# Hybrid decoder layer on one core: prompt attention issued in a fixed order on TensorE, with four smaller edits in the MLP

## The chip, the core and the metric

The kernel runs on one core of a Trainium2 chip. The metric is device time in microseconds, from the first to the last instruction and what lies around them; lower is better. The engines are TensorE (PE in the profile; its weight loads are PEld), VectorE (DVE), ScalarE (ACT), GpSimd (POOL) and SyncE (SP), whose queue issues the DMAs here.

## The reference, cut to what matters

One decoder layer is computed for a prompt of 2048 tokens and for a sample group of 8 x 8 tokens with a cache, width 1024, all in fp32. Half of the mixing is dilated attention of 8 heads of 64, in three branches (window 128 with stride 1, 512 with 4, 2048 with 16), which are merged by their softmax denominators; the other half is an RWKV-7 recurrence. Then come an output projection and an MLP.

```
n = rms_norm(x);  proj = n @ w_in
for w, d in ((128, 1), (512, 4), (2048, 16)):       # in dilated_attention
    s = q . k * scale + bias                        # keys at stride d
    mx = max(s);  e = exp(s - mx);  dn = sum(e);  o = e @ v
mall = max over branches of mx
num = sum(exp(mx - mall) * o);  den = sum(exp(mx - mall) * dn)
att = num / den
h = x + [att | rwkv] @ w_out
y = h + relu(rms_norm(h) @ w_mlp1)^2 @ w_mlp2
```

## The kernel before

The program has four stages: projections and RWKV (to some 1207 us), prompt attention (to some 1600), output projection beside the sample group's attention (to 1898), and the MLP. Apart from queues and dependencies, a list scheduler that simulates a timeline sets the order of each engine's instructions at build time: the program's order is its input, and it may put a ready instruction ahead of one that waits.

**Attention.** `attention(p, pump, ahead)` takes a pair of heads at a time, p = 0 to 3, and in it branches b = 0 to 2 and blocks of 128 queries, two at a time in branches 0 and 1 and four at a time in branch 2: 8 + 8 + 4 steps a pair. In a step, for each of the two heads `ty`: score products in two parts (`kst` and `klo`, lines 1084 and 1085, into `sc`), on VectorE a reduction that adds the bias and finds the maximum (line 1087, into `e` and `st`), the exponential on ScalarE (helper line 185), four transposes on TensorE (`pt`, line 1102), their evacuation to `pts` by `evac` (lines 1000 to 1005, in turn ScalarE and VectorE), and products with V into `o` (line 1109), which two steps (one in branch 2) share and ScalarE evacuates into `ob`.

**Merge.** `merge(p, ob, st)` is a generator. `pump()` drives it, which attention calls after each step of the next pair. It makes masked copies of the statistics on GpSimd (`zst`, `mv`, lines 1132 and 1133), brings them into rows by TensorE products (lines 1141, 1146, 1152) and ScalarE copies (`sw`), computes the branch weights on VectorE (`nall`, `scw`, `dn`, a reciprocal in line 1179), splits them into `wh` high and low, writes them to DRAM (`wD`, line 1187) and reads them back as `wrow` (line 1190). Twelve products (line 1197) spread the weights, VectorE multiplies `ob` by them, and GpSimd adds (line 1200; VectorE for the last pair). In the last pair's merge `sc` takes the place of `ax` in the names.

```
        def pump():
            for _ in range(2):
                next(before, None)
```

**MLP.** Three groups g of tokens, eight rounds r each. A round is `first` (line 1557) and `second` (line 1603), with products of high and low parts of both operands. `parts` (line 1477) splits a weight panel: `wh` on ScalarE, `wl` on VectorE, or on GpSimd where it is told so (`pooled`). `square_sums` (line 1410) squares the residual, adds on VectorE and sums by a TensorE product (line 1419) for the norm; four of its 24 calls stand at the end of group 0's round 0. `reload` fetches the next group's residual, and `normed(g + 1)` makes its scaled activations (`rl`, `mh`, `ml`) beside `second` of round 7.

Of the kernel before, what the change touches and what calls it, by code (L numbers as in the profile page):

```python
# [17 lines left out]
P = 128  # L18
# [153 lines left out]
def _build(ctx, tc, nc, I, O, dbg, upto):  # L172
# [879 lines left out]

    def attention(p, pump, ahead):
# [5 lines left out]
        for b in range(3):  # L1059
            bts = ahead.pop(("bias", p, b))  # L1060
            if p < 3:
                if b == 1:
                    ahead["kq", p + 1] = kq_load(p + 1)
                    coming = ahead["kq", p + 1][1]
                if b:
                    ahead["bias", p + 1, b - 1] = bias_load(p + 1, b - 1)
            vt = None
            for grp in range(4):
                vp, vt = vt, next_v()
                o = ppo.tile([P, 512], F32, name="o")  # L1070
                for t2 in range(0, 4, 2 if b < 2 else 4):
                    tl = [grp * 4 + t2 + i for i in range(2 if b < 2 else 4)]
                    w = 512 // len(tl)
                    work = []
                    for ty in range(2):
                        kst, klo, qst = K[ty]
                        ps = psc.tile([P, 512], F32, name="sc")
                        e = ae.tile([P, 512], F32, name="e", bufs=4)
                        blocks = []
                        for x, i in enumerate(tl):  # L1080
                            both = b < 2 and not (i == 0 if b == 0 else i < 4)
                            n = 256 if both else 128
                            c0 = x * w + w - n
                            PE.matmul(ps[:, c0:c0 + n], cols(qst, b, i, False), cols(kst, b, i, both), start=True, stop=False)  # L1084
                            PE.matmul(ps[:, c0:c0 + n], cols(qst, b, i, False), cols(klo, b, i, both), start=False, stop=True)  # L1085
                            nm, dn = st[:, 0, b, i // 4, ty, i % 4:i % 4 + 1], st[:, 1, b, i // 4, ty, i % 4:i % 4 + 1]
                            V.tensor_tensor_reduce(out=e[:, c0:c0 + n], in0=ps[:, c0:c0 + n], in1=bts[ty][:, 256 - n:256], scale=-1.0, scalar=3e38, op0=ALU.add, op1=ALU.min, accum_out=nm)
                            act(e[:, c0:c0 + n], e[:, c0:c0 + n], AF.Exp, bias=nm, scale=-1.0, accum_out=dn)
                            for hb in range(n // P):
                                old = n // P - 1 - hb  # L1090
                                if b == 0:
                                    kv = vt[:, i % 4 - old] if i % 4 >= old else vp[:, 3]
                                else:
                                    kv = (vp if old else vt)[:, i % 4]
                                blocks.append((i, kv, c0 + hb * P, hb == 0, hb == n // P - 1))
                        work.append((e, blocks))
                    ptss = []
                    for e, blocks in work:
                        pt = ppt.tile([P, 512], F32, name="pt")
                        pts = at.tile([P, 512], F32, name="pts", bufs=4)  # L1100
                        for y, (i, kv, c0, fst, lst) in enumerate(blocks):
                            PE.transpose(pt[:, y * P:(y + 1) * P], e[:, c0:c0 + P], ident)  # L1102
                        nb = len(blocks)
                        evac(pts[:, :nb * P], pt[:, :nb * P])
                        ptss.append(pts)
                    for y in range(nb):
                        for ty in range(2):
                            i, kv, c0, fst, lst = work[ty][1][y]
                            PE.matmul(o[ty * 64:ty * 64 + 64, (i % 4) * P:(i % 4 + 1) * P], kv[:, ty * 64:ty * 64 + 64], ptss[ty][:, y * P:(y + 1) * P], start=fst, stop=lst, tile_position=(0, ty * 64))  # L1109
                    pump()  # L1110
                    next(coming, None)
                if b == 0:
                    act(ob[b][:, grp * 512:(grp + 1) * 512], o, AF.Copy)
                elif b == 1:
                    act(ob[b][:, grp * 512:(grp + 1) * 512].rearrange("p (n q) -> p n q", q=4), o.rearrange("p (q n) -> p n q", q=4), AF.Copy)
                else:
                    act(ob[b].rearrange("p (m r) -> p m r", r=16)[:, :, grp * 4:(grp + 1) * 4], o.rearrange("p (r m) -> p m r", r=4), AF.Copy)
        for _ in coming:
            pass
        if p < 3:  # L1120
            ahead["bias", p + 1, 2] = bias_load(p + 1, 2)
        return merge(p, ob, st)

    def merge(p, ob, st):
# [13 lines left out]
        for x in range(2):  # L1138
            for g in range(4):
                c0 = x * 96 + g * 8  # L1140
                PE.matmul(ps[32 * g:32 * g + 32, x * P:x * P + P], flat[:, c0:c0 + 32], ident, start=True, stop=True, tile_position=(0, 32 * g))
        for x in range(2):
            for q in range(4):
                for g in range(4):
                    c0 = 256 + x * P + q * 32
                    PE.matmul(ps[32 * g:32 * g + 32, c0:c0 + 32], zst[:, x, q, g], rr1, start=True, stop=True, tile_position=(0, 32 * g))
# [3 lines left out]
        for g in range(4):  # L1150
            for ty in range(2):
                PE.matmul(ps[32 * g:32 * g + 32, 0:256], d2[:, g, ty], mv2[:, ty].rearrange("p x g c m -> p (x g c m)"), start=(ty == 0), stop=(ty == 1), tile_position=(0, 32 * g))
# [38 lines left out]
        yield  # L1191
        yield
        for g in range(4):
            cs = slice(g * 512, (g + 1) * 512)
            for b in range(3):
                ps = mp()
                PE.matmul(ps, wsel[:, g], wr[:, b], start=True, stop=True)
# [212 lines left out]
    def square_sums(h, i, c, ps, pl):  # L1410
# [7 lines left out]
        tt(sa[:, 0], sa[:, 0], sa[:, 1], ALU.add)  # L1418
        PE.matmul(ps[:SQ, 0:1], sa[:, 0], ones[:, 0:1], start=True, stop=True)
# [6 lines left out]
    with pool(name="wo2", bufs=1) as wo2, pool(name="pwo", bufs=4, space=PSUM, side="right") as pwo, pool(name="psa", bufs=1, space=PSUM) as psa, pool(name="pst", bufs=1, space=PSUM) as pst:  # L1426
# [5 lines left out]
        for c0 in range(0, NT, NC_):  # L1432
# [25 lines left out]
            if c0 + NC_ < NT:  # L1458
                for i in range(NC_ // SQ):
                    square_sums(h, c0 // SQ + i, i * SQ, pst.tile([P, 512], F32, name="pst"), wo2)  # L1460
    ph3.close()
    mw = ph4.enter_context(pool(name="mw", bufs=2))
# [5 lines left out]
    with pool(name="mm", bufs=1, side="right") as mm, pool(name="pm", bufs=8, space=PSUM) as pm:  # L1468
# [23 lines left out]
        def tmp():  # L1492
            return mw.tile([P, HT], F32, name="rl", bufs=12)
# [6 lines left out]
        def normed(g, h, mb):  # L1500
# [3 lines left out]
            dg = mw.tile([P, 8, SQ], F32, name="dg2", bufs=1)  # L1504
# [108 lines left out]
        for g in range(3):  # L1613
            late = []
            nh = None
            for r in range(8):
# [57 lines left out]
```

## Time and profile before

| | us |
|---|---|
| median of 3 runs | 3356.25 |
| lowest, highest | 3349.73, 3358.73 |
| the profiled execution | 3357.47 |
| its span | 3355.7 |
| TensorE busy in the span | 3135.5 (93%) |
| VectorE, ScalarE, GpSimd busy | 2157.2, 1469.2, 976.1 |
| mean granted TensorE clock | 0.965 |

Times in views count from the span's start. A busy total joins overlapping instructions of one engine; TensorE's products are pipelined, so the step from one start to the next is what one costs, not its duration. "idle before" names what released an engine after it had stood still.

### The profile page before, as it was taken

To read this page: it belongs to the slowest core of one execution; us is meant where nothing else is said; L and a number is where in the kernel's file an instruction comes from. 1 tells how busy PE (TensorE), PEld (TensorE's weight loads), DVE (VectorE), ACT (ScalarE), POOL (GpSimd) and SP (SyncE) were. 2 spreads that over 40 slices of the span, in tenths; PEclk is the share of its full clock that TensorE was granted. 3 is DMA by queue.
4 is the path that set the end of the run, shared out by engine and by line. 5 is a ranking of instruction groups with operands and counts; after the bars stand their busy time and mean duration, and the time that the engine had idled before them with its cause. 6 is when DMAs were issued, how large, how long until landed. Compare 5 with 4: busy or idle time off the path is not lost.

```text
span 3355.7 us, 63761 instructions
## 1 busy us (share of the span) xinstructions
PE 3135.5 (93%) x24214; PEld 2865.0 (85%) x24214; DVE 2157.2 (64%) x4547; ACT 1469.2 (44%) x3497; POOL 976.1 (29%) x1141
## 2 busy tenths in 40 slices
PE   5999899989988979999799689999999999999999
PEld 5876877877787868888688579999899999899999
DVE  4656677677566435656554577676976767967675
ACT  4545566555555446677222233232433323433332
POOL 1003422453044100111000233343533334533332
PEclk9999999999998989999899789999999999999999
DMA  5465575466456383323766322222232222222222
GB/s 169 137 185 149 131 204 158 109 157 178 124 131 178 106 279 117 126 74 90 243 221 235 123 85 89 64 85 64 98 113 64 88 63 86 88 68 84 64 89 73
DMA packets 349144, 418.55 MB, mean 125 GB/s; under 512 B 117252, under 2 KB 210367, under 8 KB 348837
## 3 DMA queue, kind: packets, MB, share of 16 engines
q1 hardware_dynamic: 348836, 414.48, 41.6%
q8 instruction: 190, 3.11, 0.4%
q14 instruction: 118, 0.96, 0.1%
HBM read 325.62 MB, written 93.46 MB: 125 GB/s over the span
## 4 chain that ended last, share of the span: by engine, by line
PE 72%; DMA 9%; DVE 9%; SPq 3%; issue 2%; POOL 2%; ACT 2%; DVEq 0%; POOLq 0%; ACTq 0%
PE pm L1603 20%; PE pm L1557 17%; PE pj L334 7%; PE pwo L1451 5%; PE pj L802 4%; PE o L1109 3%; PE pt L1102 2%; PE sc L1084 2%; PE sc L1085 2%; DVE ml L182 2%; DMA wr<-in_wq 1%; DMA wr<-in_wr 1%; DVE rl L1517 1%; DVE wl L1477 1%; DMA xg<-in_xg 1%
## 5 line engine op out<-in xcount | busy, mean ns | idle before, releaser
L185 ACT ACTIVATE wh<-wr 128x512 fp32r<-128x512 f32 x744 | 463.4, 625 | 818.5 <-PE pm L1603 473.4
L1603 PE MATMUL pm<-fh,wl 128*128 128x352 f32 x1536 | 495.9, 323 | 8.8 <-DVE wl L1477 8.8
L1603 PE MATMUL pm<-fh,wh 128*128 128x352 f32 x1536 | 493.4, 324 | 0.0
L1603 PE MATMUL pm<-fl,wh 128*128 128x352 f32 x1536 | 492.6, 323 | 0.5 <-DVE fl L182 0.5
L1557 PE MATMUL pm<-ml,wh 128*128 128x352 f32 x1344 | 437.0, 325 | 15.1 <-DVE ml L182 15.1
L1557 PE MATMUL pm<-mh,wh 128*128 128x352 f32 x1344 | 438.6, 327 | 9.4 <-ACT mh L185 9.2
L1557 PE MATMUL pm<-mh,wl 128*128 128x352 f32 x1344 | 436.0, 325 | 5.7 <-DVE wl L1477 4.6
L182 DVE TENSOR_TENSOR res<-pm,res 128x352 f32<-128x352 f32 x384 | 198.6, 522 | 287.5 <-PE pm L1603 284.7
L1477 DVE TENSOR_TENSOR wl<-wr,wh 128x512 fp32r<-128x512 f32 x432 | 361.1, 836 | 6.1 <-ACT wh L185 3.5
L1603 PEld LDWEIGHTS pm<-fh,wl 128*128 128x128 f32 x1536 | 290.2, 189 | 9.8 <-DVE wl L1477 9.8
L1603 PEld LDWEIGHTS pm<-fl,wh 128*128 128x128 f32 x1536 | 289.4, 189 | 1.3 <-DVE fl L182 1.1
L1603 PEld LDWEIGHTS pm<-fh,wh 128*128 128x128 f32 x1536 | 289.2, 189 | 0.8 <-ACT fh L185 0.2
L1557 PEld LDWEIGHTS pm<-ml,wh 128*128 128x128 f32 x1344 | 256.5, 191 | 19.1 <-DVE ml L182 19.0
L1557 PEld LDWEIGHTS pm<-mh,wh 128*128 128x128 f32 x1344 | 256.2, 191 | 11.5 <-ACT mh L185 11.5
L1557 PEld LDWEIGHTS pm<-mh,wl 128*128 128x128 f32 x1344 | 255.8, 190 | 8.9 <-DVE wl L1477 7.3
L802 PE MATMUL pj<-wh,nh 128*128 128x256 f32 (+1 forms) x816 | 242.4, 298 | 13.5 <-ACT qn L185 6.7
L802 PE MATMUL pj<-wh,nl 128*128 128x256 f32 (+1 forms) x816 | 241.1, 296 | 2.2 <-DVE nl L182 2.2
L334 PE MATMUL pj<-nh,wh 128*128 128x512 f32 (+3 forms) x600 | 222.8, 374 | 20.4 <-ACT nh L185 10.4
L1481 POOL TENSOR_TENSOR wr<-wr 128x512 f32<-128x512 f32 x48 | 68.9, 1435 | 591.0 <-DVE wl L1477 502.6
L802 PE MATMUL pj<-wl,nh 128*128 128x256 f32 (+1 forms) x816 | 240.7, 296 | 0.0
L182 DVE TENSOR_TENSOR wl<-wr,wh 128x512 fp32r<-128x512 f32 (+1 forms) x216 | 150.2, 698 | 135.2 <-ACT wh L185 130.0
L334 PE MATMUL pj<-nl,wh 128*128 128x512 f32 (+3 forms) x600 | 222.0, 371 | 5.9 <-DVE nl L182 5.9
(312 smaller groups left out, 7262.2 us busy)
## 6 DMA issues: line engine op xcount, KB each, us to landing
wr<-in_w SPq DMA_DIRECT2D x384, 256.0 KB
wr<-in_wr SPq DMA_DIRECT2D x120, 256.0 KB
wr<-in_wq SPq DMA_DIRECT2D x96, 256.0 KB
kv<-in_kc SPq DMA_DIRECT2D x40, 512.0 KB
kv<-in_vc SPq DMA_DIRECT2D x40, 512.0 KB
xsD<-xst SPq DMA_DIRECT2D x56, 256.0 KB
xrkv<-xsD SPq DMA_DIRECT2D x32, 384.0 KB
vt<-vD SPq DMA_DIRECT2D x48, 256.0 KB
```

The costliest lines, as they stand in the source:

```text
L182: V.tensor_tensor(out, a, b, op)
L185: S.activation(out, in_, func, bias=bias, scale=scale, **kw)
L334: PE.matmul(ps[:m, :n], a[:, k, :m], b[h * 4 + k][:, c0:c0 + n], start=(h == 0 and i == 0), stop=(h == 1 and i == 11))
L802: PE.matmul(out, a[h * 2 + k][:, i * P:i * P + m], b[:, k, :], start=(h == 0 and q == 0 and i % 2 == 0), stop=(h == 3 and q == 5 and (i % ...
L1084: PE.matmul(ps[:, c0:c0 + n], cols(qst, b, i, False), cols(kst, b, i, both), start=True, stop=False)
L1085: PE.matmul(ps[:, c0:c0 + n], cols(qst, b, i, False), cols(klo, b, i, both), start=False, stop=True)
L1109: PE.matmul(o[ty * 64:ty * 64 + 64, (i % 4) * P:(i % 4 + 1) * P], kv[:, ty * 64:ty * 64 + 64], ptss[ty][:, y * P:(y + 1) * P], start=fst, ...
L1451: PE.matmul(ps[:, :NC_], a[k][:, o * P:(o + 1) * P], b, start=(i == 0), stop=(i == 3 * KT - 1))
L1477: (G if pooled else V).tensor_tensor(wl, w, wh.bitcast(F32), ALU.subtract)
L1481: G.tensor_tensor(S[0], A21, A22, ALU.add)
L1557: PE.matmul(ps, a[:, k], b[:, k], start=(n == 0), stop=(n == 11))
L1603: PE.matmul(ps, a[:, f], b[:, cs], start=(i == 0), stop=(i == 11))
```

## The change

1. TensorE's instructions of the attention and the merge are issued in the program's order (`mul` and `turned`). The program now keeps a line of steps: a step's scores are issued three steps (LAG) ahead of its transposes and products with V. A step is: transposes of the step three back, `pump()`, scores of this step, `o` of the step three back, `pump()`. `e` has 6 buffers for 4. `pump()` takes one step of the merge, not two, and is called twice as often. For pairs 0 to 2 the merge yields four times, not twice, between issuing `wrow` and its first product, once for the last pair; there the line is emptied ahead of the merge.
2. ScalarE evacuates one `pt` in four, not one in two; VectorE the others.
3. The four late calls of `square_sums` are cut in two: squares and additions in round 0, TensorE's product and what follows in round 1. The `sq`, `rl` and `dg2` tiles move to a pool of their own, `mt`. `reload` comes at round 2, not 1.
4. In round 7 of groups 0 and 1, `second` makes its eight `wl` on GpSimd.

```
-        if evac.n % 2 in (0,):
+        if evac.n % 4 == 0:
...
+    def mul(*a, **k):
+        tc.keep_in_program_order(PE.matmul(*a, **k))
+    def turned(*a, **k):
+        tc.keep_in_program_order(PE.transpose(*a, **k))
+    line = []
+    def finish(step):
+        b, grp, ob, first, last, work, ptss = step
...
+        for y in range(len(work[0][1])):
+            for ty in range(2):
...
+                mul(o[ty * 64:ty * 64 + 64, ...], kv[:, ty * 64:ty * 64 + 64], ptss[ty][:, y * P:(y + 1) * P], ...)
...
+    def turn(step):
+        for e, blocks in step[5]:
+            pt = ppt.tile([P, 512], F32, name="pt")
+            pts = at.tile([P, 512], F32, name="pts", bufs=4)
+            for y, (i, old, c0, fst, lst) in enumerate(blocks):
+                turned(pt[:, y * P:(y + 1) * P], e[:, c0:c0 + P], ident)
+            nb = len(blocks)
+            evac(pts[:, :nb * P], pt[:, :nb * P])
+            step[6].append(pts)
...
+                for t2 in range(0, 4, nt_):
+                    back = line.pop(0) if len(line) == LAG else None
+                    if back:
+                        turn(back)
+                    pump()
...
-                        e = ae.tile([P, 512], F32, name="e", bufs=4)
+                        e = ae.tile([P, 512], F32, name="e", bufs=2 * LAG)
...
+                    line.append((b, grp, ob[b], t2 == 0, t2 + nt_ == 4, work, []))
+                    if back:
+                        finish(back)
                     pump()
...
+        while p == 3 and line:
+            back = line.pop(0)
+            turn(back)
+            finish(back)
         return merge(p, ob, st)
+    LAG = 3
...
-        yield
-        yield
+        for _ in range(4 if p < 3 else 1):
+            yield
...
         def pump():
-            for _ in range(2):
-                next(before, None)
+            next(before, None)
...
-                wh, wl = parts(wr)
+                wh, wl = parts(wr, last and base < 4 * HT)
...
                 if g == 0 and r == 0:
-                    for i in range(20, 24):
-                        square_sums(res, i, (i - 16) * SQ, pm.tile([P, 512], F32, name="pm"), mw)
-                if g < 2 and r == 1:
+                    sqs = [squares(res, i * SQ, mt) for i in range(4, 8)]
+                if g == 0 and r == 1:
+                    for i in range(4):
+                        square_sums(sqs[i], 20 + i, pm.tile([P, 512], F32, name="pm"))
+                if g < 2 and r == 2:
                     nh = reload(g + 1)
```

The change's line numbers are 1054 for `mul` and 1057 for `turned`, so one line stands for all of its TensorE products in the attention. Three places of the order follow: engine and place first, then rows as "line, operation, output from inputs, shape", "x8" being so many in a row.

TensorE where pair 0's last steps meet pair 1's first, the kernel before:

```order
L1109 MATMUL o<-pts,vt 64x128
L1084 MATMUL sc<-kst_15175,qst_15177 128x256
L1085 MATMUL sc<-klo_15176,qst_15177 128x256
L1109 MATMUL o<-pts,vt 64x128 x7
L1102 MATMUL pt<-ident,e 128x128
L1084 MATMUL sc<-kst_14770,qst_14772 128x128
L1085 MATMUL sc<-klo_14771,qst_14772 128x128
L1102 MATMUL pt<-ident,e 128x128
L1084 MATMUL sc<-kst_14773,qst_14775 128x128
L1085 MATMUL sc<-klo_14774,qst_14775 128x128
```

TensorE as pair 1's third step is issued, the change:

```order
L1057 MATMUL pt<-ident,e 128x128 x8
L1054 MATMUL sc<-kst_15104,qst_15106 128x256
L1054 MATMUL sc<-klo_15105,qst_15106 128x256
L1054 MATMUL sc<-kst_15104,qst_15106 128x256
L1054 MATMUL sc<-klo_15105,qst_15106 128x256
L1054 MATMUL sc<-kst_15107,qst_15109 128x256
L1054 MATMUL sc<-klo_15108,qst_15109 128x256
L1054 MATMUL sc<-kst_15107,qst_15109 128x256
L1054 MATMUL sc<-klo_15108,qst_15109 128x256
L1054 MATMUL o<-pts,vt 64x128 x8
```

Before, transposes, scores and single `o` products alternate; now a step is eight transposes, its scores, and eight `o` products.

VectorE in the change, beside pair 1's steps, from the last sum of pair 0's denominators to the low part of `wh` (`st` is the read of the maximum, `pts` the copies for `o`):

```order
L182 TENSOR_TENSOR dn<-dn,dm 128x128
L179 TENSOR_SCALAR dn<-dn 128x128
L1211 RECIPROCAL dn<-dn 128x128
L1005 COPY pts<-pt 128x384 x2
L1134 ISA e,st<-sc,bt_15110 128x256
L1134 ISA st 128x1
L182 TENSOR_TENSOR scw<-scw,dn 128x384
L1134 ISA e,st<-sc,bt_15110 128x256
L1134 ISA st 128x1
L1134 ISA e,st<-sc,bt_15112 128x256
L1134 ISA st 128x1
L182 TENSOR_TENSOR wh_15945<-scw,wh_15945 128x384
```

The copies for the next `o` products stand right behind the reciprocal, and the low part of `wh`, on which `wD` and `wrow` wait, three score reductions further on. On TensorE `ax<-mv` stands in row 5856 and the first `ax<-wrow` in row 5888; before they were rows 5922 and 6017.

TensorE at the end of the last pair, the kernel before:

```order
L1146 MATMUL sc<-mcon,zst 32x32 x10
L1102 MATMUL pt<-ident,e 128x128
L1146 MATMUL sc<-mcon,zst 32x32 x12
L1102 MATMUL pt<-ident,e 128x128
L1152 MATMUL sc<-mv_14820,mcon 32x256 x8
L1109 MATMUL o<-pts,vt 64x128 x7
L1102 MATMUL pt<-ident,e 128x128 x4
L1109 MATMUL o<-pts,vt 64x128 x8
L1257 MATMUL sc<-kv,qbd 32x256 x8
L1197 MATMUL sc<-wrow,wsel 128x512 x12
```

and in the change:

```order
L1054 MATMUL o<-pts,vt 64x128 x8
L1057 MATMUL pt<-ident,e 128x128 x8
L1054 MATMUL o<-pts,vt 64x128 x8
L1057 MATMUL pt<-ident,e 128x128 x8
L1054 MATMUL o<-pts,vt 64x128 x8
L1054 MATMUL sc<-ident,st 32x128 x8
L1054 MATMUL sc<-mcon,zst 32x32 x32
L1054 MATMUL sc<-mv_14820,mcon 32x256 x8
L1289 MATMUL sc<-kv,qbd 32x256 x8
L1054 MATMUL sc<-wrow,wsel 128x512 x12
```

The last merge's statistics stood among the last transposes and `o` products, and now stand behind all of them.

## Rows read from the trace of the kernel before

**Rows 1.** The page, part 1: busy us, share of the span, instructions

```profile
PE 3135.5 (93%) x24214; PEld 2865.0 (85%) x24214; DVE 2157.2 (64%) x4547; ACT 1469.2 (44%) x3497; POOL 976.1 (29%) x1141
```

**Rows 2.** Busy time by windows, main part of the attention (us, engines, PEclk, DMA share, GB/s)

```profile
1236.00:1585.00 349.00, 347.26 (x2711) 291.39 (x2709) 205.72 (x880) 245.64 (x852) 44.01 (x62) 0.98 0.36 114
```

**Rows 3.** Groups of TensorE's instructions, 1205 to 1236 us (busy, mean | idle before)

```profile
L1084 PE MATMUL sc<-kst,qst 128*128 128x256 f32 (+1 forms) x21 | 8.1, 401 | 5.9 <-DMA qst<-qD 5.9
L1102 PE MATMUL pt<-ident,e 128*128 128x128 f32 x29 | 7.5, 378 | 2.1 <-ACT e L185 2.1
```

**Rows 4.** Timeline of TensorE in the attention (start, us, what)

```profile
1328.25 0.43 PE L1109 MATMUL o<-pts,vt 128*64 128x128 f32 x2
1328.61 0.44 PE L1102 MATMUL pt<-ident,e 128*128 128x128 f32 x2
...
1331.38 0.66 PE L1102 MATMUL pt<-ident,e 128*128 128x128 f32 x4
1331.79 0.36 PE L1084 MATMUL sc<-kst,qst 128*128 128x256 f32 x1
...
1333.17 0.28 PE L1085 MATMUL sc<-klo,qst 128*128 128x256 f32 x1
...
1333.41 0.28 PE L1085 MATMUL sc<-klo,qst 128*128 128x256 f32 x1
...
1369.69 0.42 PE L1085 MATMUL sc<-klo,qst 128*128 128x256 f32 x1
1369.93 0.43 PE L1084 MATMUL sc<-kst,qst 128*128 128x256 f32 x1
...
1385.88 1.09 PE L1109 MATMUL o<-pts,vt 128*64 128x128 f32 x16
1386.91 0.98 PE L1102 MATMUL pt<-ident,e 128*128 128x128 f32 x7
...
1400.83 0.39 PE L1084 MATMUL sc<-kst,qst 128*128 128x128 f32 x1
1401.04 0.39 PE L1085 MATMUL sc<-klo,qst 128*128 128x128 f32 x1
```

**Rows 5.** Timeline by tile and line, merge beside pair 1 (durations, start us)

```profile
L185 ACT ACTIVATE sw<-ax x1: 383/383/383, 1319.5 to 1319.5; 128x256 f32<-128x256 f32 x1
...
L1197 PE MATMUL ax<-wrow,wsel x1: 480/480/480, 1344.2 to 1344.2; 128*128 128x512 f32 x1
```

**Rows 6.** Timeline of all engines, end of the attention

```profile
1597.43 0.88 DVE L182 TENSOR_TENSOR scw<-nall,sw 128x128 f32<-128x128 f32 x3
...
1597.81 1.09 PE L1109 MATMUL o<-pts,vt 128*64 128x128 f32 x14 [1.49 <-ACT pts L185]
...
1605.00 0.55 DVE L182 TENSOR_TENSOR wh<-scw,wh 128x384 fp32r<-128x384 f32 x1
...
1613.27 1.19 PE L1197 MATMUL sc<-wrow,wsel 128*128 128x512 f32 x2 [13.37 <-DMA wrow<-wD]
```

**Rows 7.** Busy time by windows, after that wait and in two places of the MLP

```profile
1605.00:1629.00 24.00, 13.71 (x32) 9.21 (x33) 15.64 (x30) 2.64 (x5) 0.00 (x0) 0.50 0.29 97
1898.00:1947.00 49.00, 24.58 (x74) 18.73 (x72) 44.24 (x67) 17.75 (x37) 27.55 (x17) 0.58 0.21 62
2400.00:2436.00 36.00, 26.90 (x147) 24.40 (x146) 35.87 (x54) 14.67 (x29) 22.89 (x17) 0.95 0.42 142
```

**Rows 8.** TensorE's waits, 1990 to 2006 us (us, times, longest)

```profile
PE pm L1419 <- DVE sq L182: 6.8, 3, 3.2
```

**Rows 9.** Timeline of VectorE there

```profile
2000.32 1.18 DVE L182 TENSOR_TENSOR sq<-sq 128x352 f32<-128x352 f32 x3 [0.37 <-ACT sq L185]
```

**Rows 10.** The page, part 5

```profile
L1603 PE MATMUL pm<-fh,wl 128*128 128x352 f32 x1536 | 495.9, 323 | 8.8 <-DVE wl L1477 8.8
```

**Rows 11.** Timeline by tile, `wl`, 2000 to 3300 us (ns least/median/most)

```profile
L1477 DVE TENSOR_TENSOR wl<-wr,wh x397: 676/692/1781, 2010.6 to 3299.0; 128x512 fp32r<-128x512 f32 x199
L1477 POOL TENSOR_TENSOR wl<-wr,wh x89: 1283/1342/1618, 2008.5 to 3297.2; 128x512 fp32r<-128x512 f32 x89
```

More of the change, by code (lines that the diff above doesn't have):

```diff
@@ L1051, in next_v @@
         return vq.pop(0)
+    def mul(*a, **k):
[5 more added lines that the diff above has]
+        b, grp, ob, first, last, work, ptss = step
+        if first:
+            finish.old = finish.vt if grp else None
+            finish.vt = next_v()
+            finish.o = ppo.tile([P, 512], F32, name="o")
+        o, vt, vp = finish.o, finish.vt, finish.old
+        for y in range(len(work[0][1])):
+            for ty in range(2):
+                i, old, c0, fst, lst = work[ty][1][y]
+                if b == 0:
+                    kv = vt[:, i % 4 - old] if i % 4 >= old else vp[:, 3]
+                else:
+                    kv = (vp if old else vt)[:, i % 4]
+                mul(o[ty * 64:ty * 64 + 64, (i % 4) * P:(i % 4 + 1) * P], kv[:, ty * 64:ty * 64 + 64], ptss[ty][:, y * P:(y + 1) * P], start=fst, stop=lst, tile_position=(0, ty * 64))
+        if not last:
+            return
+        if b == 0:
+            act(ob[:, grp * 512:(grp + 1) * 512], o, AF.Copy)
+        elif b == 1:
+            act(ob[:, grp * 512:(grp + 1) * 512].rearrange("p (n q) -> p n q", q=4), o.rearrange("p (q n) -> p n q", q=4), AF.Copy)
+        else:
+            act(ob.rearrange("p (m r) -> p m r", r=16)[:, :, grp * 4:(grp + 1) * 4], o.rearrange("p (r m) -> p m r", r=4), AF.Copy)
+    def turn(step):
[7 more added lines that the diff above has]
+            step[6].append(pts)
     def attention(p, pump, ahead):
@@ L1066, in attention @@
                     ahead["bias", p + 1, b - 1] = bias_load(p + 1, b - 1)
-            vt = None
             for grp in range(4):
[L1069 to L1072, printed above, removed]
+                nt_ = 2 if b < 2 else 4
+                for t2 in range(0, 4, nt_):
[3 more added lines that the diff above has]
+                    pump()
+                    tl = [grp * 4 + t2 + i for i in range(nt_)]
                     w = 512 // len(tl)
@@ L1089, in attention @@
                             for hb in range(n // P):
[L1090 to L1095, printed above, removed]
-                        work.append((e, blocks))
[L1097 to L1109, printed above, removed]
+                                blocks.append((i, n // P - 1 - hb, c0 + hb * P, hb == 0, hb == n // P - 1))
+                        work.append((e, blocks))
+                    line.append((b, grp, ob[b], t2 == 0, t2 + nt_ == 4, work, []))
+                    if back:
+                        finish(back)
                     pump()
                     next(coming, None)
[L1112 to L1117, printed above, removed]
         for _ in coming:
@@ L1196, in merge @@
                 ps = mp()
[L1197 removed]
+                mul(ps, wsel[:, g], wr[:, b], start=True, stop=True)
                 tt(ob[b][:, cs], ps, ob[b][:, cs], ALU.mult)
@@ L1417, in square_sums @@
         tt(sa[:, :2], sa[:, :2], sa[:, 2:], ALU.add)
-        tt(sa[:, 0], sa[:, 0], sa[:, 1], ALU.add)
-        PE.matmul(ps[:SQ, 0:1], sa[:, 0], ones[:, 0:1], start=True, stop=True)
+        q = hp.tile([P, SQ], F32, name="sqs", bufs=4)
+        tt(q, sa[:, 0], sa[:, 1], ALU.add)
+        return q
+    def square_sums(sq, i, ps):
+        PE.matmul(ps[:SQ, 0:1], sq, ones[:, 0:1], start=True, stop=True)
         V.tensor_copy(ssq[i // 8][:SQ, i % 8:i % 8 + 1], ps[:SQ, 0:1])
```

19 lines of the change are left out of this document (10 added, 9 removed).

## The prediction

> **What bounds the kernel now.** I read the busy totals first: TensorE is busy for 93% of the span [rows 1], so what counts is what its instructions cost and the few places where it waits. In the windows, TensorE is busy for 347.26 of the 349 us of the main attention stretch at a clock of 0.98, with VectorE at 206 and ScalarE at 246 [rows 2]: nothing is waited for, yet the time depends on how the instructions are mixed. Before 1236 us it waits for loads of Q instead [rows 3]. The timeline shows what mixing costs [rows 4]: eight `o` products in a row (16 records) take 1.03 us from the first start to the next kind's, while one alone (2 records) takes 0.36. Today's order breaks groups as 7 + 1 and the like, 144 groups of `o` where the new order has 79, and puts transposes between score products. So: see in rows 4 the start-to-start steps, not the durations, which overlap.
>
> **The attention's rate.** From rows 4: four transposes ahead of scores take 0.41 us, and each further one 0.11, so eight take 0.85; branch 0's score products follow at 0.12, branch 1's at 0.24, branch 2's at 0.22; I add 0.2 for each change into and out of scores. A step of branch 0 is 0.85 + 8 x 0.12 + 0.2 + 1.03 = 3.0 us, of branch 1 4.0, of branch 2 (16 score products) 5.6. A pair has 8, 8 and 4 of them: 78.4, less some 2.5 for the first steps, which have half the blocks: 75.9; four pairs are 304. By 1236 us 21 of 384 score pairs and 29 of 600 transposes are done [rows 3], 5%; I let the change be as far then, since that stretch is paced by the loads: on SP's queue six of pair 0's 24 K and Q loads, which stood ahead of the other loads, now stand behind them, which could cost up to the 5.9 us that TensorE waits for Q today, or nothing; I take nothing, since the loads in all are the same. 95% of 304 is 289; three merges, at some 5 us of TensorE each (an estimate: 12 weight products at a third of a us and the statistics), make 304, at a clock of 0.98 310. Undisturbed the last `o` would end at 1546 where it now ends near 1599 [rows 6]: 53 us to be had. The unknown is what the order, now fixed, makes TensorE wait for.
>
> **The merge's waits.** Today the list scheduler fills the time between the statistics and the weight products with whatever is ready; the merge beside pair 1 takes from the second `sw` at 1319.5 to the first L1197 at 1344.2, 24.7 us [rows 5], and nothing waits. In the new order, from the `mv` products to the first weight product there stand four groups of transposes and three of scores and `o`: 3.0 + 2.6 + 3.0 + 0.85 = 9.4 us. The chain takes longer: at the end of the attention, where it meets only some other work on VectorE, `scw` starts at 1597.43 and the low part of `wh` ends at 1605.55, 8.1 us, plus 0.9 for `sw` and `nall`; the two transfers behind it (`wD`, then `wrow`) land at 1613.27, another 7.7 [rows 6]. That is 16.7 against 9.4: TensorE stands still for 7.3 us. VectorE's order puts seven score reductions and, behind the reciprocal, the copies that step 3's `o` products need among the chain, so part of that comes early; I take 8 for each of pairs 1 to 3, 24 us. The ends are nothing, and 24.7 - 9.4 = 15.3 each. What is queued behind the waiting weight product is all of TensorE's work, and behind that ScalarE's exponentials. SP's queue issues `wD` and `wrow` one behind the other in both kernels; K and Q loads stand in front of them either way.
>
> **The clock behind the waits.** After the 13.37 us wait at the end of the attention [rows 6] TensorE was granted half its clock, 1.2 instead of 2.4 GHz, over the whole window of 24 us [rows 7]. A shorter wait in two pieces should bring a shorter dip; I take 3 us per pair, 9 in all, between nothing and 12 each (half of 24). For **evacuations**, three in four now on VectorE: some 40 more copies on an engine with 143 us free in 349 [rows 2]; the free time hides them, and I take 3 us for moments where it doesn't, between nothing and 32 (0.4 a step). Six buffers of `e` instead of four only feed the three-step lag. Sum: 310 + 24 + 9 + 3 = 346 from 1236, last `o` at 1582, 17 us earlier.
>
> **The end of the attention.** Now the last merge's statistics lie among pair 3's last steps, and `wrow` lands 14.5 us after the last `o` (1613.27 against 1598.8). In the new order the three steps in the line are drained first; statistics take about 2, the chain 16.7 as above: 19. Cost 5 us, between 3 and 7; the twelve weight products behind it are the same.
>
> **The MLP.** The products of the last four square sums move a round later: TensorE's 6.8 us wait for `sq` in three pieces [rows 8] goes, and its next user, the second round's first product, is late for nothing that I see. Gain 6.8. At the head of the MLP, where VectorE is busy for 44.24 of 49 us [rows 7], the new order has three of these groups of additions ahead of work that TensorE waits for, 1.18 us each [rows 9]: cost 3, between nothing and 4. The `reload` a round later, the separate pool and the four small `sqs` tiles cost nothing: the reload has five rounds left.
>
> Sixteen low parts go from VectorE to GpSimd, eight in the last round of each of two groups. VectorE is full there, 35.87 of 36 us [rows 7], and TensorE waits 8.8 us on such low parts in the whole MLP [rows 10]: that is the most to be gained. One takes 1342 ns on GpSimd and 692 on VectorE [rows 11]; GpSimd, at 22.89 of 36, gets 8 x 1.34 = 10.7 more and is nearly full, and it makes the next group's sums too. If each arrives later by the difference, 16 x 0.65 = 10.4 us are lost. I take a gain of 1, near the middle.
>
> **Sum:** 17 - 5 + 6.8 - 3 + 1 = 17 from the profiled execution's 3357.5 gives 3340.5; the median of the runs is 1.2 lower, so 3339. A measurement can tell about 0.3%, 10 us, from no change.
>
> **The rivals.**
> - Forecast, 3339 (0.47), its own range 3326 to 3352.
> - The weights come in time (0.18). If the chain runs faster than at the end, or TensorE is late by itself, the 24 + 9 us go: 3306. For it: today the chain shares VectorE with TensorE's full rate. Against it: 7.7 us for two transfers alone nearly fill the 9.4.
> - GpSimd and VectorE block each other at the group ends (0.15). A low part on GpSimd then holds up VectorE for all its length, instead of freeing it: 10.4 us lost instead of 1 won, 3350. For it: the same low part takes 676 ns at least and 1781 at most on VectorE [rows 11]. Against it: the median of 692 lies at the least, while GpSimd works through much of the MLP. The Trainium skill states such a rule, "SBUF — State Buffer", section "SBUF: two separate sides": a GpSimd instruction and a VectorE one with two SBUF inputs take a shared port pair as an exclusive lock, and the other blocks. The row's 1781 agrees with it, the median speaks against its being met often.
> - Long waits and half the clock (0.10), the side that is slower: the merges' waits are 15.3 us each, as long as today's chain makes them, and each is followed by 24 us at half clock as in rows 7: 3 x (7.3 + 9) = 49 more, 3388. It decides from a wait of about 13 us in one piece, as at the end now. Against it: two pieces, and a dip in the attention need not be bound by the clock alone.
> - The order doesn't help, as each step waits (0.10): with the order fixed, TensorE can't go round a late `pts` or `e`; 0.4 us in each of 80 steps is 32, so 3339 - 3 + 32 = 3368. Against it: transposed blocks are three steps old, and VectorE has the room.
>
> **How the numbers follow.** 3304 to 3368 holds the forecast, the weights in time and the blocked group ends, 0.8; both slow rivals lie at its edge or outside. Faster than 3346: 0.40 of the forecast, 0.18, and 0.04 of the third: 0.62. Slower than 3366: the two slow ones less a little, 0.17. Between: 0.21.
>
> **What would show it.** Right: `o` groups of 16 records and almost none of 2; the last `o` near 1582; TensorE's waits with three of some 5 us for `wrow` and three of some 3 for `pts`, each with a clock row at half behind it; `sq` gone from the waits; L1197 in the last merge some 19 us after the last `o`. Wrong: weights without a wait (first rival), VectorE's low parts and `ml` well above 692 ns at the group ends (second), windows at 0.5 of 20 us behind each merge (third), waits for `pts` in every step (fourth). The forecast falls if a step of branch 0 takes more than 3.5 us.

## The result, and the profile after

The change is slower: 3601.05 us, median of 4 runs (3600.16 to 3601.91), against 3354.12 for the kernel before beside it; the ratio is 1.0736, 95% interval 1.0717 to 1.0755. The forecast was 3339, the range's upper end 3368.

The stages of both kernels, read off TensorE's first and last products in the two traces, show where it went (us):

| stage | before | change |
|---|---|---|
| first score product | 1207.8 | 1219.3 |
| last `o` ends | 1598.9 | 1844.1 |
| from there to the first product of the output projection | 24.3 | 27.1 |
| output projection and sample attention | 275.5 | 270.8 |
| MLP, first to last product | 1451.7 | 1452.3 |

All of it lies in the prompt attention. Totals of the page and its row of the granted clock in 40 slices, of the change, and behind them the clock row of the kernel before:

```profile
PE 3249.4 (90%) x24214; PEld 2943.8 (82%) x24214; DVE 2193.5 (61%) x4571; ACT 1472.9 (41%) x3457; POOL 997.1 (28%) x1157
...
PEclk9999999999989757676769988999999999999999
...
PEclk9999999999998989999899789999999999999999
```

Slices 14 to 21, the attention, fall to 5 to 7 tenths; before, its slices were at 8 and 9. The attention stretch by windows (us, then busy time of PE, PEld, DVE, ACT, POOL, then PEclk, DMA share, GB/s):

```profile
1240.00:1844.00 604.00, 470.40 (x2833) 380.14 (x2832) 255.10 (x952) 264.78 (x854) 46.38 (x66) 0.69 0.22 69
```

It answers to [rows 2], where TensorE was idle for 1.7 of 349 us at a clock of 0.98. Here it is idle for 604 - 470.4 = 133.6 us, and its work, the same instructions, is 115 us longer than the 355 that the kernel before is busy from 1240 to 1599 us, at a clock of 0.69. Most of the longer work is transposes and `o` products: in the change's trace a transpose follows the one before by 0.11 us at the full granted clock and by 0.22 at half of it, a record of `o` by 0.06 and 0.10, while the score products of branches 1 and 2 keep their 0.24 and 0.22 at either level. Which instructions waited, TensorE's groups of that stretch (busy, mean ns | idle before, releaser):

```profile
L1054 PE MATMUL o<-pts,vt 128*64 128x128 f32 x1188 | 131.1, 386 | 2.7 <-ACT pts L185 1.7 <-issue 0.8 <-DVE pts L1005 0.2
L1057 PE MATMUL pt<-ident,e 128*128 128x128 f32 x586 | 122.1, 375 | 0.0
L1054 PE MATMUL sc<-kst,qst 128*128 128x256 f32 x201 | 90.6, 456 | 78.8 <-DVE st L1134 77.7 <-DMA klo<-klD 1.1
L1054 PE MATMUL sc<-kst,qst 128*128 128x128 f32 x166 | 75.5, 455 | 52.7 <-DVE st L1134 52.7
```

The idle time lies in front of one kind, the first part of a score product, and its releaser is `st`, the reduction on VectorE; no group waits for `pts` or `wrow` worth speaking of. Counted from the first score product on (us, times, longest):

```profile
PE sc L1054 <- DVE st L1134: 134.5, 222, 2.2
```

The same kind in the kernel before, 1236 to 1585 us:

```profile
L1084 PE MATMUL sc<-kst,qst 128*128 128x256 f32 x197 | 82.1, 425 | 0.1
...
L1084 PE MATMUL sc<-kst,qst 128*128 128x128 f32 x161 | 65.8, 409 | 0.0
```

0.1 us there, 130 here. A piece of branch 2 in the change, TensorE and VectorE by time (start, us; in brackets the idle time before):

```profile
1353.18 0.29 DVE L1134 CUSTOM_DVE_ANT_0 e<-sc,bt 128x128 f32<-128x128 f32 x1 [0.79 <-PE sc L1054]
1353.39 0.08 DVE L1134 DVE_READ_ACCUMULATOR2_ANT st<- 128x1 f32 x1
...
1353.53 0.29 PEld L1054 LDWEIGHTS sc<-kst,qst 128*128 128x128 f32 x1 [0.58 <-DVE st L1134]
...
1353.82 0.41 PE L1054 MATMUL sc<-klo,qst 128*128 128x128 f32 x1
...
1354.26 0.29 DVE L1134 CUSTOM_DVE_ANT_0 e<-sc,bt 128x128 f32<-128x128 f32 x1 [0.79 <-PE sc L1054]
1354.48 0.08 DVE L1134 DVE_READ_ACCUMULATOR2_ANT st<- 128x1 f32 x1
...
1354.62 0.29 PEld L1054 LDWEIGHTS sc<-kst,qst 128*128 128x128 f32 x1 [0.58 <-DVE st L1134]
```

See the chain: a product ends, the reduction reads it, the next product starts 0.06 us after that reduction has ended, and so on; 1.09 us per product where [rows 4] have steps of 0.22 for each of its two parts. The products in question go to different columns of the same tile `ps`, one PSUM bank. In the program each block's reduction stands right behind its product, and the next block's product, which the framework lets into the tile only when the reduction has read it, waits. A head has two blocks in a step, or four in branch 2, so the program holds 224 such products (56 a pair), and the trace 222 such waits. A tile `ps` fills one bank, so no run here tells a wait for the bank from a wait for the tile. The Trainium skill has a rule that fits, in "PSUM — Partial Sum Buffer", section "PSUM bank collisions raise a hardware error": a bank that two engines use at once (in the same partitions) is an error, so accesses are to be guarded by bank and not by address. The rows agree with such a guard: disjoint columns, and still a wait.

### The profile page after: what moved, and what is told of

It reads as the page before. It is cut to its first block, busy times and chain, and to the rows that moved or that the text cites. A ratio compares the mean times of both kernels' runs of the same rounds, so it can differ in the third digit from the quotient of the medians.

```text
span 3599.8 us, 63788 instructions
## 1 busy us (share of the span) xinstructions
PE 3249.4 (90%) x24214; PEld 2943.8 (82%) x24214; DVE 2193.5 (61%) x4571; ACT 1472.9 (41%) x3457; POOL 997.1 (28%) x1157
## 4 chain that ended last, share of the span: by engine, by line
PE 62%; DVE 10%; DMA 6%; issue 2%; SPq 2%; POOL 2%; ACT 1%; DVEq 0%; ACTq 0%; POOLq 0%
PE pm L1641 19%; PE pm L1595 17%; PE pwo L1487 5%; PE sc L1054 5%; PE o L1054 3%; PE pj L334 3%; PE pj L802 3%; PE pt L1057 3%; DVE e L1134 2%; DVE ml L182 1%; DVE rl L1555 1%; DMA wr<-in_wq 1%; DVE pts L1005 1%; PE ax L1054 1%; SPq L847 0%
## 5 line engine op out<-in xcount | busy, mean ns | idle before, releaser
L1515 DVE TENSOR_TENSOR wl<-wr,wh 128x512 fp32r<-128x512 f32 x416 | 347.6, 836 | 6.5 <-ACT wh L185 3.2
L1054 PE MATMUL sc<-kst,qst 128*128 128x256 f32 (+1 forms) x384 | 174.7, 458 | 145.0 <-DVE st L1134 134.5
L185 ACT ACTIVATE e<-e,st 128x256 f32<-128x256 f32 (+1 forms) x384 | 176.7, 460 | 231.2 <-DVE st L1134 229.1
L1134 DVE CUSTOM_DVE_ANT_0 e<-sc,bt 128x256 f32<-128x256 f32 (+1 forms) x384 | 138.2, 365 | 212.7 <-PE sc L1054 202.4
L1054 PEld LDWEIGHTS sc<-kst,qst 128*128 128x128 f32 x384 | 107.7, 280 | 194.1 <-DVE st L1134 184.2
L802 PE MATMUL pj<-wh,nh 128*128 128x256 f32 (+1 forms) x816 | 241.6, 297 | 10.4 <-ACT qn L185 8.1
```

The source lines that it names most:

```text
L185: S.activation(out, in_, func, bias=bias, scale=scale, **kw)
L802: PE.matmul(out, a[h * 2 + k][:, i * P:i * P + m], b[:, k, :], start=(h == 0 and q == 0 and i % 2 == 0), stop=(h == 3 and q == 5 and (i % ...
L1054: tc.keep_in_program_order(PE.matmul(*a, **k))
L1515: (G if pooled else V).tensor_tensor(wl, w, wh.bitcast(F32), ALU.subtract)
```

## The experiments

**Products ahead of reductions.** The change, with one edit:

```
                             mul(ps[:, c0:c0 + n], ..., klo ..., start=False, stop=True)
+                        for x, i in enumerate(tl):
+                            both = b < 2 and not (i == 0 if b == 0 else i < 4)
+                            n = 256 if both else 128
+                            c0 = x * w + w - n
                             nm, dn = ...
                             V.tensor_tensor_reduce(...)
```

> The change, with one edit: the score products of all blocks of a head are issued ahead of that head's reductions on VectorE, so TensorE's order stays as it is, but the second block's product no longer waits for the first block's reduction, which reads the same PSUM bank; the reduction waits for the product instead. Theory (same-bank wait): TensorE's 134.5 us of waiting for VectorE ahead of score products fall under 15, the clock in the attention goes back above 0.9, the last o comes at 1580 to 1620 instead of 1844, and the time is 3340 to 3380. Rival (VectorE, with three in four evacuations, paces each step): the waits move but the last o stays after 1780, time over 3530. Rival (the clock falls by itself, from the regular pauses of a fixed order): the clock stays under 0.8, time over 3480.

3372.49 us, ratio 1.0044 (1.003 to 1.0058): 229 of the 247 us are back, with TensorE's order as it was. Its waits in the attention (us, times, longest):

```profile
PE ax L1054 <- DMA wrow<-wD: 27.8, 3, 12.0
PE sc L1054 <- DMA qst<-qD: 12.6, 3, 9.7
PE o L1054 <- DVE pts L1005: 3.1, 5, 2.4
PE o L1054 <- ACT pts L185: 1.8, 1, 1.8
PE o L1054 <- issue: 0.8, 2, 0.6
PE sc L1054 <- DVE st L1138: 0.7, 1, 0.7
```

134.5 us for `st` have become 0.7, so the cause is shown: the wait for the bank, not VectorE's load and not the fixed order by itself. What is left of waits is mainly what I had forecast, three for `wrow` of 27.8 us together (24 forecast), and those for the first Q. A step of branch 1 at full clock and the windows of the whole attention, of branch 1 and of branch 2 in pair 0:

```profile
1270.59 1.09 PE L1054 MATMUL o<-pts,vt 128*64 128x128 f32 x16
1271.62 1.09 PE L1057 MATMUL pt<-ident,e 128*128 128x128 f32 x8
1272.46 0.58 PE L1054 MATMUL sc<-kst,qst 128*128 128x256 f32 x1
```

```profile
1240.00:1622.00 382.00, 348.46 (x2821) 310.44 (x2817) 235.28 (x950) 234.29 (x853) 46.55 (x66) 0.88 0.36 114
1260.00:1280.00 20.00, 20.00 (x157) 17.63 (x156) 13.25 (x54) 14.23 (x52) 0.55 (x3) 1.00 0.11 29
1284.00:1312.00 28.00, 28.00 (x192) 25.76 (x195) 12.55 (x72) 17.13 (x74) 1.57 (x4) 0.76 0.37 122
```

Eight `o` products 1.03 us, eight transposes 0.84: as summed. But branch 2, without a wait, has 0.76 of the clock.

**Heads in turn.** The change, its loop over blocks outside and over heads inside:

```
-                    for ty in range(2):
+                    for x, i in enumerate(tl):
...
-                        for x, i in enumerate(tl):
+                        for ty in range(2):
```

> The change, with the two heads' score products alternating, each block's reduction issued right behind its product as in the change. Two products of one bank then have one product of the other bank between them. Same-bank wait: the wait per block shrinks by the other product's 0.24 us and the two heads' waits overlap, so about half of the 245 us comes back: 3450 to 3530. VectorE paces each step: no gain, 3590 to 3610. Clock by itself: as VectorE, over 3560.

3421.63 us, ratio 1.0187 (1.0164 to 1.021). The wait is still there and smaller:

```profile
PE sc L1054 <- DVE st L1135: 32.3, 72, 1.2
PE sc L1054 <- DMA qst<-qD: 12.0, 2, 10.4
PE ax L1054 <- DMA wrow<-wD: 11.6, 3, 6.3
```

It falls from 134.5 to 32 us by putting one product of the other bank between; 179 us come back, more than the half that I expected, and the time lies below the expected 3450. The dose agrees with the bank, and the clock follows the wait: of 180 us only 102 are waits.

**Low parts back on VectorE.** `scores_first` with

```
-                wh, wl = parts(wr, last and base < 4 * HT)
+                wh, wl = parts(wr)
```

> The same edit as scores_first, and the sixteen low parts of the last rounds back on VectorE. If GpSimd makes them late, as rounds 6 to 8 of the change took 3.1 and 4.4 us more than before at the two group boundaries, this is 6 to 9 us faster than scores_first; if the boundaries are longer for another reason (reload a round later), it is within 2 us of it.

3365.41 us, ratio 1.0022 (1.0008 to 1.0036), 7.1 less than `scores_first`. From TensorE's first product in a group's last round to that in the next group's second round it takes 132.1 and 131.8 us in `scores_first` (132.1 and 132.0 in the change), and 129.0 and 127.4 here, as before (129.0, 127.6). So GpSimd's low parts cost the change 7.5 us. They don't cost it where they are made: at the two boundaries the last round takes 60.4 and 64.0 us in the change against 65.5 and 64.7 before, and the next group's first round 71.7 and 68.0 against 63.5 and 62.9. TensorE's waits at the first boundary, two stretches of the kernel before (last round, next round) and one of the change (next round; in its last round 0.5 us is the longest):

```profile
PE pm L1603 <- DVE wl L1477: 4.6, 2, 3.2
...
PE pm L1557 <- DVE wl L1477: 2.5, 3, 1.1
PE pm L1557 <- DVE ml L182: 1.9, 2, 1.4
...
PE pm L1595 <- DVE wl L1515: 4.2, 2, 3.9
PE pm L1595 <- DVE ml L182: 3.7, 1, 3.7
```

The wait for low parts in the last round is gone, as the edit meant, but a round later TensorE waits longer for VectorE, at a clock of 0.90 for 1.00. In the change the low parts by engine, to be held against [rows 11]:

```profile
L1515 DVE TENSOR_TENSOR wl<-wr,wh x402: 673/693/1746, 2145.8 to 3539.0; 128x512 fp32r<-128x512 f32 x134
L1515 POOL TENSOR_TENSOR wl<-wr,wh x108: 1285/1498/2369, 2167.4 to 3500.8; 128x512 fp32r<-128x512 f32 x108
```

Those on GpSimd are longer than before, median 1498 against 1342 and most 2369 against 1618; those on VectorE are not. VectorE's `ml` is, though: in the last round of the second boundary its median is 1251 ns against 834 before. So it is VectorE's work that comes late in the next round; whether GpSimd holds it up was not tried.

**The MLP's edits alone,** the attention as before:

```
 attention, merge, evac and pump as before; square sums, reload and wl as in the change
```

> The kernel before, with the edits of the MLP alone (square sums in two parts, reload at round 2, low parts on GpSimd). By the stages of the two traces the MLP is 0.6 us longer from its first to its last product: 3350 to 3358, no change. If part of the 245 us came from the MLP, or from its other placement of buffers, over 3370.

3356.89 us, ratio 0.9997 (0.9985 to 1.001): nothing, the sum of a gain and a loss. The square sums bring 6.1 us up to the second round (103.9 us from the MLP's first product before, 97.9 in the change) and 1.6 in it (59.6, 58.0); GpSimd's low parts take it back.

**Branch 2 mixed.** `scores_first_wl_vector`, where branch 2 turns one head, makes a head's eight products, turns the other:

```
-                        turn(back)
+                        turn(back, slice(0, 1 if b == 2 else 2))
...
+                        if ty and b == 2:
+                            turn(back, slice(1, 2))
                         kst, klo, qst = K[ty]
```

> scores_first_wl_vector (3365), with branch 2's step cut in halves: four transposes, eight score products, four transposes, eight score products, then the o products, in place of eight, sixteen, eight. Work is the same. In scores_first branch 2's steps take 7.0 us, with granted clocks of 0.54 and 0.97 in turn and no wait, where rows at full clock add to 5.6. Theory (the sixteen 128-wide score products in a row leave TensorE so lightly used that the clock falls): mixing them lifts the clock in branch 2 and its steps to 5.6 to 6.2, 13 to 22 us less, 3343 to 3352. Rival (the clock falls because the products are narrow, in whatever order): steps stay at 7, 3362 to 3368.

In `scores_first` a step of branch 2 reads (TensorE, start, us):

```profile
1284.16 1.85 PE L1054 MATMUL o<-pts,vt 128*64 128x128 f32 x16
1285.94 1.95 PE L1057 MATMUL pt<-ident,e 128*128 128x128 f32 x8
1287.56 0.44 PE L1054 MATMUL sc<-kst,qst 128*128 128x128 f32 x1
1287.81 0.39 PE L1054 MATMUL sc<-klo,qst 128*128 128x128 f32 x1
1288.03 0.39 PE L1054 MATMUL sc<-kst,qst 128*128 128x128 f32 x1
```

`o` and transposes run at half speed (1.78 and 1.62 us for what takes 1.03 and 0.84), after sixteen narrow products at steps of 0.22; 7.0 us for the step. Mixed, in the like place:

```profile
1281.20 1.09 PE L1054 MATMUL o<-pts,vt 128*64 128x128 f32 x16
1282.22 0.66 PE L1057 MATMUL pt<-ident,e 128*128 128x128 f32 x4
...
1284.42 0.62 PE L1057 MATMUL pt<-ident,e 128*128 128x128 f32 x4
...
1286.68 1.09 PE L1054 MATMUL o<-pts,vt 128*64 128x128 f32 x16
```

5.48 us from one group of `o` to the next. Some steps still meet half the clock (0.85 from 1275 to 1297 us, against 0.76 above). By runs it is 3359.28, ratio 1.0005 (0.9989 to 1.0021): 6 us less than without it, with intervals that overlap. The profiled executions differ by 16.5, of which 5 are an earlier first score product; the expected 13 to 22 is not shown by this pair. The mechanism is shown in part: from the first to the last score product of branch 2, the four pairs added up, the traces of the three kernels without the mixing have 98.7, 94.9 and 91.4 us, those of the six with it 83.6 to 90.8. But the order doesn't decide it alone. In `lag2`, mixed, pairs 0 and 1 take 6.7 us a step at a clock of 0.78; in `weights_later`, not mixed, some steps take 5.5.

**Weight products later.** `scores_first_wl_vector` with

```
-        for _ in range(4 if p < 3 else 1):
+        for _ in range(8 if p < 3 else 1):
...
-                yield
+                if b:
+                    yield
```

> scores_first_wl_vector (3365), with the merge yielding eight times ahead of the first weight product, not four, and only after every second and third of a group's three weight products, so that they end where they ended. TensorE's waits for wrow, 27.8 us in three in scores_first, lie behind 9.4 us of work; two more steps are 6.2 us more of it. Theory (the waits are the chain's 16.7 us less the work ahead): 3 x 6 = 18 us less of waiting and some 3 to 9 us of clock behind it, less 1 us for each pair of products on the one bank, 3340 to 3352. Rival (the wait only moves to the buffer of ob, which the next pair's branch 1 writes): within 5 us of 3365.

3370.3 us, ratio 1.0046 (1.003 to 1.0062): nothing gained, a miss. The wait for `wrow` did shrink:

```profile
PE ax L1054 <- DVE ob L182: 10.9, 12, 1.3
PE ax L1054 <- DMA wrow<-wD: 6.7, 3, 2.6
```

`wrow` 6.7 us for the 29.1 of `scores_first_wl_vector`, but of two weight products in a row the second waits until VectorE has read `ax`, a single bank, 10.9 us in twelve, and the waits of `o` for `pts` grow from 4.4 to 12.1 us. So the waits moved: the time is the rival's (within 5 us of 3365), though not the place. Again one bank and the engine that reads it.

**Both.**

> Both edits. If the gains are independent, the sum of the two: 3325 to 3342, below the kernel before. If the clock's loss in branch 2 and the merge's waits overlap, 3340 to 3352.

3355.85 us, ratio 0.9997 (0.9988 to 1.0007): as the kernel before, short of the sum of two gains of which one wasn't there. Against `weights_later`, from which only the mixing sets it apart, it is 14.5 us less, and the intervals don't touch: here the mixing brings the 13 to 22 that it was expected to.

**The kernel before with products ahead of reductions.**

> The kernel before with the one edit alone (products of a head's blocks ahead of its reductions), order left to the scheduler. Theory (the list scheduler goes round the same-bank wait, so that it costs it little): 3340 to 3362, within 0.5% of before; what it gains are contiguous groups. Rival (the same wait costs the kernel before much too, in split groups): under 3335.

3374.51 us, ratio 1.0064 (1.0048 to 1.0081): slower, outside both expectations. That the bank's wait cost the kernel before little is seen in its own row above (0.1 us); lifting it brought nothing, since the scheduler, given other dependencies, made another order, whose last `o` ends at 1613.2. From the first score product to there TensorE is idle for 7 us more than before and has a clock of 0.91 for 0.96; what in the order brings that was not settled.

**A lag of two steps.** `branch2_split` with

```
-    LAG = 3
+    LAG = 2
```

> branch2_split (3359) with a lag of two steps for three, so that e has four buffers as in the kernel before. In the change the first score product comes at 1219 and not at 1208, and all K and Q loads of pair 0 stand behind the last projection's stores in SP's queue. Theory (the two more buffers of e push K's buffers onto memory that the projections still hold, so the loads start late): six loads go ahead again, the first score product comes at 1206 to 1212, and 6 to 11 us are won, 3348 to 3354. Rival (the fixed order on TensorE delays the start): the first score product stays after 1217 and the time within 4 us. If two steps are too short for the exponential, waits for e or pts of over 10 us appear and it is slower.

3354.07 us, ratio 0.9988 (0.9978 to 0.9998): 5 us below `branch2_split`, a little short of the 6 to 11, with intervals that overlap. SP's issues of `kst` from 1175 to 1215 us, the change and then `lag2` (durations; first and last start):

```profile
L1019 SPq DMA_DIRECT2D kst<-khD x2: 430/504/579, 1212.3 to 1214.3; - x2
```

```profile
L1019 SPq DMA_DIRECT2D kst<-khD x5: 376/423/527, 1181.7 to 1213.1; - x5
```

The loads begin at 1181.7 again and not at 1212.3, and the first score product at 1208.7 (in `branch2_split` they were at 1207.7 and 1214.5). That fits the buffers of `e`: with six, K's tiles would have to wait for memory that the projections hold, which no run shows by itself. The lag was changed with the buffers, so the two are not told apart; a fixed order alone doesn't delay the start.

**The last merge's statistics earlier.** `lag2`, where for p == 3

```
+            while line:
+                back = line.pop(0)
+                turn(back)
+                finish(back)
+                next(rest)
```

> lag2 with the last merge's statistics issued among the last two steps that are drained, and not behind them. TensorE waited 13.4 us for wrow there in branch2_split, in a stretch of 28 us from the last o to the output projection (24.3 before). Theory (the chain from the statistics to wrow sets the end): 2 to 5 us less than lag2. Rival (something else, as GpSimd's masked copies, sets it): within 1 us.

3355.6 us, ratio 0.9994 (0.9981 to 1.0006): no gain. From the last `o` to the output projection it is 26.9 us and not 29.9, but the last `o` ends 2.3 later, since the statistics now stand ahead of it.

**Nine, and eleven yields.** One weight product per yield, branch 1 and 0 of each group first, then branch 2:

```
-        for _ in range(4 if p < 3 else 1):
+        for _ in range(9 if p < 3 else 1):
...
+            seq = [(g, b) for g in range(4) for b in (1, 0)] + [(g, 2) for g in range(4)]
```

> lag2_tail with nine yields ahead of the weight products of pairs 0 to 2, one product per yield again, and in the order that frees ob of branch 1 first (branches 1 and 0 of each group, then branch 2). In weights_later the wait for wrow fell from 27.8 us to 6.7 but came back as 10.9 us of waiting between two products on one bank. Theory: without the doubled products waits for wrow fall under 5 us and nothing takes their place: 15 to 27 us less than lag2_tail, 3322 to 3336, faster than the kernel before. Rival (the wait moves to ob's single buffer or to the clock): within 6 us of lag2_tail.

3342.71 us, ratio 0.9949 (0.9932 to 0.9965); the waits for `wrow` are 11.2 us and not the under 5 expected. With eleven yields and without the last edit of the tail:

> lag2_tail_weights9 (3343) without the tail's edit and with eleven yields ahead of the weight products. What was left there were three waits for wrow of 2 to 4 us each, 11.2 us together, and 12 us at half clock behind them. Theory: one more step of 3 to 4 us ahead of them takes most of these waits, 5 to 10 us less, 3333 to 3339. Rival (the weight products now end a step later than the next pair's branch 1 writes ob, so ScalarE waits for it and TensorE for ScalarE): 3340 to 3350.

3321.77 us, ratio 0.9899 (0.9882 to 0.9915): faster than the kernel before by 34 us and than the change by 279. Waits and window:

```profile
PE sc L1054 <- DMA wrow<-wD: 15.5, 1, 15.5
PE o L1054 <- DVE pts L1005: 9.4, 10, 4.3
PE sc L1054 <- DMA qst<-qD: 2.2, 1, 2.2
...
PE ax L1054 <- DMA wrow<-wD: 0.2, 1, 0.2
```

```profile
1240.00:1567.00 327.00, 319.42 (x2749) 283.87 (x2751) 224.65 (x929) 223.28 (x831) 46.58 (x66) 0.97 0.39 123
```

`wrow` is waited for at the end alone, the clock is at 0.97, the last `o` ends at 1567.0. The gain of 21 us over nine yields is twice the expected 5 to 10. In the traces 4.8 us of it are an earlier first score product; most of the rest lies between that and the last `o`, where the waits of 11.2 us are gone and the clock is 0.95 for 0.93. The tail's edit went out in the same run, so its share is not told apart.

## Why the prediction was wrong

- **The step that failed** is the first one, the rate: "branch 0's score products follow at 0.12, branch 1's at 0.24, branch 2's at 0.22". Those steps of [rows 4] are right for products whose bank is free. The list scheduler had put only such products side by side; I took the step for a property of the product and gave it to an order in which every second product (three in four in branch 2) waits for a reduction on VectorE. In the change a step takes a median of 5.8, 7.2 and 11.3 us in branches 0, 1 and 2, where I had 3.0, 4.0 and 5.6; by my own sign, 3.5 in branch 0, the forecast falls. The term that the sum lacked, at nothing without a reason, was this wait: 134.5 us, and nearly as much in slower work behind it. I looked up what each change of kind costs, not what each row of the new order depends on. The wait was there to be found: in the program the reduction stands between two products into one tile. The order itself came as forecast: 68 groups of `o` with 16 records and none with 2, where there had been 67.
- "nothing is waited for" in [rows 2] was read as slack. It was the scheduler's order, which had other rows to put between two products of a bank; the fixed order has none there.
- The fourth rival, "the order doesn't help, as each step waits", named the way but not the wait (`pts`, `e`) nor the size: 0.4 us a step against 133.6 / 80 = 1.7, and nearly as much again in slower work. The third, half the clock, came true at another place, in each step and not behind merges.
- **With the bank's wait gone** the rate's terms held: `scores_first` has steps of 3.00 to 3.05 us at the end of pair 0's branch 0, where no merge runs beside them, and of 4.04 in branch 1 (3.0 and 4.0 summed). Branch 2 took 7.0 for 5.6, by the clock, and 5.5 where the clock held. Its last `o` comes at 1622 for the forecast 1582; the late start (15.8), branch 2 (16 x 1.4 = 22) and the longer waits for `wrow` (3.8) add up to 42 of these 40 us.
- **Merge's waits:** 24 us forecast, 27.8 in three in `scores_first`. They came in one piece of 7.9, 7.9 and 12.0 us and not in two, and half the clock lasted for 4 to 4.6 us behind each, which makes some 7 us lost (half of 13) where I had 9; waits for `pts` were 4.9 us where I had 3. In the change itself pairs 1 to 3 don't wait for `wrow`; that fits its slow steps, which give the chain more time. The working was right in the main, and it could be used: eleven yields take the waits of pairs 1 to 3 away.
- **Start:** "I take nothing" for the moved loads. It was 11.5 us, twice the bound of 5.9, which I took from what TensorE waited for today, not from how late the loads would go out. In the other kernels with a lag of three the first score product comes between 1214.5 and 1223.5.
- **End:** 5 forecast, 2.8 measured in the change (27.1 against 24.3).
- **MLP:** the square sums, 6.8 less 3 forecast, brought 6.1 and 1.6: the 3 at the head were not paid in full. The low parts on GpSimd, +1 forecast, cost 7.5, inside the bound of 10.4, but not by a late arrival: the wait that was to go went, and VectorE's `ml` and `wl` came late a round on. The second rival was near in size; of its signs `ml` showed at one boundary and `wl` did not, and no run settles it.
- The 4.7 us that the output projection's stage is shorter in the change weren't explained; in the other kernels it lies between 266 and 276.

## What to carry to other kernels

In this trace, which a scheduler had ordered, a step from one start to the next was the price of an instruction whose inputs are there; before an order is fixed, write down for each row what it depends on, PSUM bank by PSUM bank, and how far behind that stands. Where several products go to one bank in a fixed order, issue all of them ahead of the first reader: here one added loop header was worth 229 us. With the order left to the scheduler the same edit cost 18 us. A wait of TensorE cost its length here and then the clock behind it, so the fixed order paid only when its longest chain had enough rows in front of its end (eleven yields).

## What the runs showed that I had not expected

The clock nearly doubled the damage: about 130 us of pauses, none over 2.2 us, came with 115 us of slower work at a mean clock of 0.69, though TensorE was busy for 78% of the stretch. And TensorE can lose its clock without any pause: sixteen 128-wide score products in a row, busy 28.00 of 28 us by the profile, had 0.76 of it in branch 2, while branch 1's eight 256-wide ones held 1.00. Width is not all that sets them apart: branch 2 reads its keys and queries at a stride of 16, branch 1 of 4, and a transpose of 128 columns takes half the step. Mixing transposes among them made the loss rarer and did not end it.
